# Re-pricing GpSimd's operations in the planner of a two-layer recurrent decoder step

## The chip, the cores and the metric

The kernel runs on one NeuronCore of a Trainium2 chip. TensorE multiplies matrices, VectorE (DVE), ScalarE (ACT) and GpSimd (POOL) do the elementwise work, and SyncE (SP) issues most of the transfers between device memory and the on-chip memory. Each engine runs its own instruction queue in order and waits on semaphores for the others. The metric is the device time of one execution in microseconds (us).

## The reference

The reference computes one inference step of a decoder trunk with two layers on 1024 prompt tokens and 8 x 4 sampled tokens, 1056 columns in all, with 1024 features. Everything is float32.

- Layer 0 is an RG-LRU layer: RMS norm, a projection to 2 x 1536 features (recurrent branch and gate), a causal convolution over 4 positions, two block-diagonal gate products with sigmoids, the recurrence h = a h + b over time, a multiplication by silu(gate), an output projection and the residual.
- Layer 1 is an HGRN2 layer: RMS norm, a projection to 4 x 1024 features (q, f, value, gate) for 8 heads, a gated linear recurrence with a 128 x 128 state per head, computed in chunks, a norm per head, a multiplication by silu(gate), an output projection and the residual.
- A final RMS norm follows. The outputs are the two activations and the new states of both layers.

## The kernel before

Activations are held transposed, features on the 128 partitions and tokens along the columns, in three chunks of 352 columns (`CH`). Every large product is made of three fp32r products (`mm3`, L243 to L245): an operand is split into a rounded part `hi` and the rest `lo`, and hi x hi, hi x lo and lo x hi are added up in PSUM. For each weight tile this takes a load (SP), a cast on ACT that makes `hi` (L378, and L1428 in `seven`) and a subtract that makes `lo`. That subtract runs on GpSimd nearly always (`subtract` with `e` as G, L323); activations get theirs from DVE mostly.

Layer 0 runs in the order: first products of gates and convolution inputs chunk by chunk while the inputs arrive (`begin`, `products`), then four groups of 384 recurrent features (`conv`, `gate`, `lru`, `split_y`) woven with the output products (`out`, `out_last`), and the first three products of layer 1 (`first1`). Layer 1 computes two heads with ordinary products and the other six with a seven-product scheme in place of eight (`seven`), whose combined operands are built on DVE, ACT and GpSimd where the layers meet (`build`: sums at L1368, casts at L1371, subtracts at L323). Each head has four bursts of small products (`burst1` to `burst4`): decay scalings of DVE (L1034, L1043, own gate L1064), 32-column products (L1052, L1106), transposes (L1161), states (L1217) and outputs (L1271, L1273). The end is the output projection, the final norm and the writing of the rows (`finish`: DVE L1701 for most rows, ACT and GpSimd L1699 for the last three of a block).

No instruction is issued where it is written. Each layer has one `Flow`: `fl.add` records an engine, an assumed duration, what is read and written, a priority and the code that emits it. The helpers `act`, `dve`, `pool` and `dma` compute the assumed duration from the number of columns n. `Flow.run` then simulates the queues. `plan` goes forward in time: at each step the engine that is free first takes, of its ready operations, the one with the least key. `back` goes backward from the end with the durations that the forward pass took and gives each operation its latest start, which is the next key. This alternates eight times (`TURNS`), and the plan with the earliest end is kept; for layer 0 the end is that of TensorE's last operation. For layer 0 `search` then tries 3000 random shifts of the keys of operations planned in the first 60 us, with a fixed seed, and keeps those that do not delay the first TensorE operation planned more than 20 us after that. Operations come out in the order of the kept plan, and with `manual_schedule` that is the order of each engine's queue. Large products are chained by `main=True`, so their order among themselves is fixed; small ones of layer 0 without it are placed by the plan. A `both` operation of DVE is planned to last until GpSimd's current operation ends and then nearly its own duration again, where GpSimd is busy at its start. The two layers are planned separately, each from an idle machine.

The change is in `pool`, L318 to L319. It sets the planned duration of weight and activation subtracts (L323), adds and squares in layer 0 (L428, L433, L582), gate maps (L720, L1010, L1012), masked values (L1195), the copies of a few columns and the last rows (L1699, L1735). The rsqrt operations on GpSimd (L447, L1299, L1670) have their own constants and do not go through it.

Of the kernel before, what the change touches and what calls it, by code (L numbers as in the profile page):

```python
# [211 lines left out]
def tile_trunk(ctx: ExitStack, tc: tile.TileContext, xT, prm, hc, w0, wg, wo0, w1, wo1, s_in,  # L212
# [83 lines left out]
    with ExitStack() as l0:  # L296
        pl = l0.enter_context(tc.tile_pool(name="l0", bufs=1, reuse_waits="tile"))
        fl = Flow("PE")
# [17 lines left out]
            fl.add("DVE", 0.13 + 0.0011 * n, emit, r, w, prio, both=both)  # L316

        def pool(n, emit, r, w, prio=5):  # L318
            fl.add("POOL", 0.1 + 0.00245 * n, emit, r, w, prio)  # L319

        def subtract(e, n, b, x, a, r, w, prio):

            emit = lambda: e.tensor_tensor(b, x, a.bitcast(F32), op=ALU.subtract)  # L323
            if e is G:
                pool(n, emit, r, w, prio)
            else:
                dve(n, emit, r, w, prio, True)
# [95 lines left out]
        def squares(k, x, xk, acc, eng=None, own=None, mult=False):  # L423

            a, ak = acc
            sq, sk = next(own or ts) if k else acc
            if mult:
                pool(CH, lambda: G.tensor_tensor(sq[:, :CH], x, x, op=ALU.mult), (xk,), (sk,), 2)  # L428
            else:
                act(CH, lambda: S.activation(sq[:, :CH], x, AF.Square), (xk,), (sk,), 2)  # L430
            if k:
                e = eng or G
                (pool if e is G else dve)(CH, lambda: e.tensor_tensor(a[:, :CH], a[:, :CH], sq, op=ALU.add), (sk, ak), (ak,), 2)  # L433
# [28 lines left out]
        def conv(g, head=False):  # L462

            items = []
            for j in range(3):
# [3 lines left out]
                def evac(c, ps, pk, by=None, j=j, m=m, mine=mine):  # L469
                    n = CH if c < 2 else 1024 - 2 * CH  # L470
                    if c == 0:
                        mine[0] = next(xbs)
                        pool(3, lambda xb=mine[0][0]: G.memset(xb[:, :3], 0.0), (), (mine[0][1],), 2)
                    elif head:
                        mine[c] = next(xbs)
                        pool(3, lambda xb=mine[c][0]: G.tensor_copy(xb[:, :3], tails[:, 4 * j:4 * j + 3]), (("tail", j),), (mine[c][1],), 0)
# [450 lines left out]
    with ExitStack() as l1:  # L927
        p1 = l1.enter_context(tc.tile_pool(name="l1", bufs=1, reuse_waits="tile"))
        fl = Flow(side=0.4)
# [637 lines left out]
        for k in range(H):  # L1567
            if k < 4:
                olds = [("x", 1, k, x) for x in range(2)] + [("T", 1, i, k, x) for i in range(2) for x in range(2)]
            else:  # L1570
                n, i = ((2, 0), (3, 0), (4, 0), (4, 1))[k - 4]
# [241 lines left out]
```

## Time and profile before

| | |
|---|---|
| time, median of 3 runs | 1061.05 us (1060.89 to 1061.98) |
| profiled execution: its time | 1062.88 us |
| profiled execution: span from first to last instruction | 1061.1 us |
| TensorE busy / weight loads busy | 1051.4 us (99%) / 1025.8 us (97%) |
| DVE / ACT / GpSimd busy | 843.7 us (80%) / 588.2 us (55%) / 542.0 us (51%) |
| mean granted TensorE clock | 0.995 |
| moved from and to device memory | 103.07 MB, mean 97 GB/s |

A row of a group reads: line, engine, operation, output <- inputs with their shapes, count | busy time, mean duration of one in ns | idle time of the engine before them and what ended it. A row of the time order reads: start, duration, engine, line, operation, tiles, count, and in brackets the idle time before it and what ended that. A row of the waits reads: who waited <- for whom: total us, times, longest. Lines are those of the kernel. PE is TensorE, PEld its weight loads.

### The profile page before, as it was taken

The page shows a single profiled execution, that of the slowest core. Times are in us where ns is not written, and L with a number is a line of the kernel's source. Part 1 is how long each engine was busy: PE and PEld are TensorE (multiplying, and loading weights), DVE is VectorE, ACT ScalarE, POOL GpSimd, SP SyncE. Part 2 cuts the span into 40 slices and gives each one's busy share as a digit, 9 for nine tenths or more (in the row PEclk, how much of TensorE's full clock was granted, in tenths as well). Part 3 has the DMA queues.
Part 4 walks back from the last instruction along what each step waited for, and adds up shares of the span by engine and source line. Part 5 has one row for each costly group of instructions (what it writes and reads, how often), then busy time and mean ns, then how long its engine had stood idle before and what let it go on. Part 6 is the DMA issues. An engine that isn't in the chain of part 4 may idle for free.

```text
span 1061.1 us, 25695 instructions
## 1 busy us (share of the span) xinstructions
PE 1051.4 (99%) x9972; PEld 1025.8 (97%) x9972; DVE 843.7 (80%) x1677; ACT 588.2 (55%) x1329; POOL 542.0 (51%) x604
## 2 busy tenths in 40 slices
PE   9999999999999999999999999999999999999997
PEld 9999999999999999999999999999999999999996
DVE  7999996888888689265799988978879797994435
ACT  6568656867675875243354474646464645652323
POOL 3425443444444455555677656555555565642544
PEclk9999999999999999999999999999999999999997
DMA  9201112123742685440210131312121212354204
GB/s 301 64 26 45 54 51 74 57 61 108 240 150 61 182 287 165 133 130 28 73 51 30 44 101 45 101 37 89 44 83 53 85 58 74 113 181 156 85 1 164
DMA packets 70121, 103.07 MB, mean 97 GB/s; under 512 B 9200, under 2 KB 51184, under 8 KB 70000
## 3 DMA queue, kind: packets, MB, share of 16 engines
q1 hardware_dynamic: 67696, 98.67, 29.9%
q10 hardware_dynamic: 2304, 2.77, 0.8%
q8 instruction: 78, 1.28, 0.5%
q14 instruction: 43, 0.35, 0.1%
HBM read 71.05 MB, written 25.49 MB: 91 GB/s over the span
## 4 chain that ended last, share of the span: by engine, by line
PE 89%; DVE 7%; POOL 1%; DMA 1%; issue 1%; ACT 0%; POOLq 0%; ACTq 0%; DVEq 0%
PE mm L243 24%; PE mm L244 24%; PE mm L245 24%; PE hg L567 1%; PE hg L1052 1%; PE hg L1161 1%; PE hg L1271 1%; DVE R L1368 1%; PE hg L1217 1%; PE hg L243 1%; PE hg L244 1%; PE hg L245 1%; PE hg L1273 1%; DMA wraw<-in_w_dram 1%; DVE tmp L1368 1%
## 5 line engine op out<-in xcount | busy, mean ns | idle before, releaser
L243 PE MATMUL mm<-xh,whi 128*128 128x352 f32 (+1 forms) x1143 | 358.8, 314 | 0.0
L245 PE MATMUL mm<-xh,wlo 128*128 128x352 f32 (+1 forms) x1143 | 353.4, 309 | 0.0
L244 PE MATMUL mm<-xl,whi 128*128 128x352 f32 (+1 forms) x1143 | 353.4, 309 | 0.0
L323 POOL TENSOR_TENSOR wlo<-wraw,whi 128x256 fp32r<-128x256 f32 (+3 forms) x184 | 203.2, 1121 | 178.7 <-ACT whi L378 79.9
L244 PEld LDWEIGHTS mm<-xl,whi 128*128 128x128 f32 x1143 | 215.3, 188 | 1.5
L243 PEld LDWEIGHTS mm<-xh,whi 128*128 128x128 f32 x1143 | 215.0, 188 | 1.5
L245 PEld LDWEIGHTS mm<-xh,wlo 128*128 128x128 f32 x1143 | 215.0, 188 | 0.0
L499 DVE SCALAR_TENSOR_TENSOR k<-xb,prm_sb,k 128x352 f32<-128x352 f32 (+2 forms) x144 | 90.0, 636 | 10.9 <-ACT k L496 7.7
L243 PE MATMUL mm<-t,whi 128*128 128x264 f32 (+1 forms) x306 | 89.4, 292 | 0.0
L244 PE MATMUL mm<-t,whi 128*128 128x264 f32 (+1 forms) x306 | 87.8, 287 | 0.0
L245 PE MATMUL mm<-t,wlo 128*128 128x264 f32 (+1 forms) x306 | 87.6, 286 | 0.0
L1501 DVE TENSOR_TENSOR k<-mm,k 128x264 f32<-128x264 f32 x144 | 60.2, 426 | 20.6 <-PE mm L245 17.5
L323 POOL TENSOR_TENSOR wlo<-R,whi 128x256 fp32r<-128x256 f32 x64 | 60.0, 957 | 24.7 <-ACT whi L1428 24.7
L582 POOL TENSOR_TENSOR k<-X 128x352 f32<-128x352 f32 x36 | 43.9, 1228 | 47.8 <-DVE R L583 38.2
L378 ACT CAST whi<-wraw 128x512 fp32r<-128x512 f32 (+2 forms) x83 | 46.1, 574 | 30.0 <-PE mm L244 15.7
L243 PEld LDWEIGHTS mm<-t,whi 128*128 128x128 f32 x306 | 57.7, 188 | 0.2
L245 PEld LDWEIGHTS mm<-t,wlo 128*128 128x128 f32 x306 | 57.8, 189 | 0.0
L244 PEld LDWEIGHTS mm<-t,whi 128*128 128x128 f32 x306 | 57.7, 189 | 0.0
L1428 ACT CAST whi<-wraw 128x512 fp32r<-128x512 f32 x52 | 32.1, 619 | 36.3 <-PE mm L245 16.8
L243 PE MATMUL mm<-yh,whi 128*128 128x352 f32 x153 | 50.0, 327 | 0.0
L245 PE MATMUL mm<-yh,wlo 128*128 128x352 f32 x153 | 49.4, 323 | 0.0
L244 PE MATMUL mm<-yl,whi 128*128 128x352 f32 x153 | 49.4, 323 | 0.0
(479 smaller groups left out, 2640.9 us busy)
## 6 DMA issues: line engine op xcount, KB each, us to landing
wraw<-in_w_dram SPq DMA_DIRECT2D x90, 256.0 KB, 2.8
wraw<-in_wo_dram SPq DMA_DIRECT2D x34, 192.0 KB, 2.6
si<-in_s_in_dram SPq DMA_DIRECT2D x8, 512.0 KB, 3.6
out_ss_out_dram<-si SPq DMA_DIRECT2D x8, 512.0 KB, 2.6
R<-in_w_dram SPq DMA_DIRECT2D x15, 256.0 KB, 2.6
sg<-x1b SPq DMA_DIRECT2D x21, 176.0 KB, 3.0
x<-sg SPq DMA_DIRECT2D x21, 176.0 KB, 1.9
R<-td SPq DMA_DIRECT2D x72, 44.0 KB, 2.0
```

Of the source, the lines that this page charges most:

```text
L243: T.matmul(out, wh, xh, start=first, stop=False)
L244: T.matmul(out, wh, xl, start=False, stop=False)
L245: T.matmul(out, wl, xh, start=False, stop=last)
L323: emit = lambda: e.tensor_tensor(b, x, a.bitcast(F32), op=ALU.subtract)
L378: act(m, lambda hi=hi, raw=raw, m=m: S.copy(hi[:, :m], raw[:, :m]), rk, (hk,), prio)
L499: dve(u, lambda src=src, dst=dst, sh=sh, k=k: V.scalar_tensor_tensor(dst, sh(src, k), pc("cw", 12 * k + m), dst, op0=ALU.mult, op1=ALU.add ...
L567: fl.add("PE", 0.62, lambda ps=ps, i=i, c=c: T.matmul(ps[:96, :CH], gs[:, i, :], ST[:96, chunk(c)], start=True, stop=True), (("gs",), *((" ...
L582: pool(CH, lambda x=x, a=a, b=b: G.tensor_tensor(x, a.bitcast(F32), b.bitcast(F32), op=ALU.add), (ak, bk), (xk,), 3)
L1052: T.matmul(ps[32 * j:32 * j + 32, n * w:n * w + w], B[:, o:o + 32], q(slice(o, o + 32)), start=True, stop=True, tile_position=(0, 32 * j))
L1368: dve(n, lambda: V.tensor_tensor(o, a, b, op=op), r, (w,), prio, True)
L1428: act(512, lambda: S.copy(hi, raw), (rk,), (hk,), 2)
L1501: dve(QT, lambda: V.tensor_tensor(o[0], z[0], u[0], op=ALU.add), (z[1], u[1]), (o[1],), 0)
```

## The change

One line in the helper that records a GpSimd operation. Below 96 columns the assumed duration stays at 0.1 + 0.00245 n us; from 96 columns on it is 0.42 + 0.00195 n us.

```diff
@@ -316,7 +316,7 @@
         def pool(n, emit, r, w, prio=5):
-            fl.add("POOL", 0.1 + 0.00245 * n, emit, r, w, prio)
+            fl.add("POOL", 0.1 + 0.00245 * n if n < 96 else 0.42 + 0.00195 * n, emit, r, w, prio)
```

No instruction, operand or buffer is changed. What can differ is the order of the instructions in each engine's queue, in both layers.

## The prediction

> **What bounds the kernel now.** I read the page first: busy shares, DMA shares and the chain that ended last.
>
> ```profile
> PE 1051.4 (99%) x9972; PEld 1025.8 (97%) x9972; DVE 843.7 (80%) x1677; ACT 588.2 (55%) x1329; POOL 542.0 (51%) x604
> PE 89%; DVE 7%; POOL 1%; DMA 1%; issue 1%; ACT 0%; POOLq 0%; ACTq 0%; DVEq 0%
> ```
>
> TensorE is 99% busy, weight loads fill 97%, and TensorE holds 89% of the chain. GpSimd, whose assumed durations change, is busy half the time and holds 1%. A busy matmul says little, since records overlap, so I looked at starts in the time order, for two waits of TensorE:
>
> ```profile
> 30.82 0.32 PE L244 MATMUL mm<-xl,yh 128*128 128x352 f32 x1
> 30.98 0.32 PE L245 MATMUL mm<-xh,yl 128*128 128x352 f32 x1
> 31.98 0.42 PE L243 MATMUL mm<-xh,yh 128*128 128x352 f32 x1 [0.68 <-DVE sg L527]
> ...
> 565.67 0.32 PE L245 MATMUL mm<-xh,wlo 128*128 128x352 f32 x1
> 566.42 1.44 PE L1052 MATMUL hg<-R,a 128*32 128x64 f32 x62 [0.43 <-DVE R L1064]
> ```
>
> Each record lasts 0.32 us, yet starts are 0.16 us apart. A stall therefore shows as the step beyond that: 1.00 us instead of 0.16 at 30.98, that is 0.84 lost, and 0.75 instead of 0.16 at 565.67, 0.59 lost. All that TensorE waited for in the whole span:
>
> ```profile
> PE hg L728 <- DVE ones L255: 1.0, 1, 1.0
> PE mm L243 <- DVE sg L527: 0.7, 1, 0.7
> PE hg L1106 <- DVE a L1034: 0.5, 1, 0.5
> PE hg L277 <- ACT sg L1726: 0.4, 1, 0.4
> PE hg L1052 <- DVE R L1064: 0.4, 1, 0.4
> ```
>
> Five waits, 3.0 us. The first is before the warm-up matmuls and no order changes it. That leaves 2.0 us: 0.7 in the start, 0.9 where the layers meet, 0.4 in the end. The stretches say the same (time, busy PE, PEld, DVE, ACT and POOL with counts, clock, DMA share, GB/s):
>
> ```profile
> 0.00:20.00 20.00, 18.97 (x134) 18.97 (x135) 14.91 (x34) 13.22 (x28) 7.54 (x13) 1.00 0.91 299
> ...
> 60.00:505.00 445.00, 445.00 (x2740) 438.56 (x2739) 347.42 (x602) 284.16 (x556) 211.53 (x233) 1.00 0.37 110
> 505.00:570.00 65.00, 63.95 (x804) 62.19 (x803) 57.19 (x100) 28.79 (x67) 47.35 (x43) 1.00 0.18 55
> 570.00:960.00 390.00, 390.00 (x5447) 376.74 (x5447) 339.55 (x738) 210.57 (x557) 216.26 (x250) 1.00 0.25 80
> ...
> 1045.00:1061.00 16.00, 9.27 (x56) 8.21 (x54) 6.63 (x16) 3.73 (x9) 5.67 (x7) 0.65 0.46 162
> ```
>
> For 835 of 1061 us (60 to 505, 570 to 960) TensorE has no gap at all. The stretches where the order can matter are the first 60 us (transfers at 0.91 of the engines), the meeting of the layers (DVE 57.19 of 65, GpSimd 47.35 of 65, its highest share), and the last 16.
>
> **The change part by part.** No instruction, tile or transfer is added or removed. One price in the planner changes: a GpSimd operation on n at least 96 columns is planned at 0.42 + 0.00195 n us instead of 0.1 + 0.00245 n. What moves is the position of instructions in each engine's queue, SP's loads among them, since the plan emits them all. Old price, new price and row:
>
> ```profile
> L323 POOL TENSOR_TENSOR wlo<-wraw,whi 128x256 fp32r<-128x256 f32 x104 | 93.9, 924 | 76.8 <-ACT whi L1428 62.1 <-DVE k L1501 14.6
> L323 POOL TENSOR_TENSOR wlo<-wraw,whi 128x512 fp32r<-128x512 f32 x58 | 83.3, 1443 | 87.3 <-ACT whi L378 65.3 <-DMA sg<-x 11.9 <-DVE X L505 3.9
> L582 POOL TENSOR_TENSOR k<-X 128x352 f32<-128x352 f32 x36 | 43.9, 1228 | 47.8 <-DVE R L583 38.2 <-DVE X L505 7.3 <-DVE nr L440 1.9
> L433 POOL TENSOR_TENSOR xb<-xb,k 128x352 f32<-128x352 f32 x21 | 20.4, 971 | 22.8 <-ACT k L430 22.6
> L1195 POOL TENSOR_TENSOR vb<-vst,bm 96x256 fp32r<-96x256 f32 x32 | 24.6, 785 | 25.0 <-DVE vst L1177 17.7 <-PE hg L1246 7.1 <-PE mm L1246 0.2
> ```
>
> At 256 columns 0.727 becomes 0.919 (measured 0.924); at 512, 1.354 becomes 1.418 (1.443); at 352, 0.962 becomes 1.106 (1.228 at L582). These prices improve. But L433 at 352 columns was right and becomes 0.14 too long, and L1195 moves from 0.06 short to 0.13 long. So one formula in n fits most of GpSimd's time and misfits some. An operation flagged `both` on DVE is also planned to stand still while GpSimd works, so longer GpSimd prices make the planned DVE slower as well.
>
> (1) The steady stretches, 60 to 505 and 570 to 960. TensorE waits for nothing, so no order can gain: 0. The cover is GpSimd's own earliness: the first row above shows 62.1 us of idling before 256-column subtracts because ACT had not yet cast, so those subtracts follow their input at once. If the cover went, a subtract run one place later would cost up to its own 0.92 us at the product that needs it. DVE has 50 us of air in 390. Bounds 0 to +0.9; I take 0.
>
> (2) The start. The search over the first 60 us draws from a fixed seed, but its draws fall on other neighbours once the planned times differ, so another order of loads is likely. A weight load and the transfer rate:
>
> ```profile
> wraw<-in_w_dram SPq DMA_DIRECT2D x90, 256.0 KB, 2.8
> ```
>
> 262,144 bytes at the 299 GB/s of the first stretch take 0.88 us. If the load that TensorE needs next falls behind one other, that is +0.88, ahead of one, -0.88; two such places bound it at -1.8 and +1.8. Nothing tells the sign, so I take 0. The casts and the subtracts follow their loads and count within that shift.
>
> (3) The wait on L527. DVE is late there after sums that run beside GpSimd; the queue of both around it:
>
> ```profile
> 26.88 2.69 DVE L433 TENSOR_TENSOR R<-R,xo 128x352 f32<-128x352 f32 x3
> 29.91 1.14 DVE L433 TENSOR_TENSOR R<-R,xo 128x352 f32<-128x352 f32 x2
> 30.98 0.52 DVE L527 TENSOR_TENSOR sg<-mm,R 128x352 f32<-128x352 f32 x1
> ...
> 26.86 1.69 POOL L323 TENSOR_TENSOR yl<-wraw,yh 128x512 fp32r<-128x512 f32 x1 [2.75 <-ACT yh L378]
> ```
>
> Three sums took 2.69 us while a subtract of 1.69 ran, two took 1.14 later. A plan that knows the subtract is longer may put L527 before sums that nobody needs yet. Between -0.7 (gone) and +0.7 (the same again) I take -0.35: this is the wait that the corrected price bears on most directly.
>
> (4) The meeting of the layers. Here DVE is the second limit. Rows of both engines:
>
> ```profile
> 538.58 0.67 DVE L1034 TENSOR_TENSOR sg<-sg 128x512 f32<-128x512 f32 x1
> 543.70 1.78 DVE L1034 TENSOR_TENSOR a<-a,sg 128x512 f32<-128x512 f32 x1
> ...
> 541.74 3.19 POOL L323 TENSOR_TENSOR wlo<-wraw,whi 128x512 fp32r<-128x512 f32 x2
> 564.10 0.82 POOL L1010 TENSOR_SCALAR ST<-k,smalls 128x352 f32<-128x352 f32 x1
> 564.91 2.42 POOL L1012 TENSOR_SCALAR a<-k,smalls 128x352 f32<-128x352 f32 x1
> ...
> 563.43 0.98 DVE L1368 TENSOR_TENSOR tmp<-xh,tmp 128x264 f32<-128x264 f32 x1 [1.10 <-POOL t L323]
> ```
>
> A 512-column multiply of DVE takes 0.67 us alone and 1.78 while GpSimd subtracts: 1.11 us for a collision. DVE's queue ahead of L1064 and L1034 holds the sums of the layer's operands, and behind it wait four scalings, the masks and the evacuations. Best case both waits vanish: -0.9. Worst case four scalings of one level that ran free collide: 4 x 1.11 = 4.4, less the 1.10 at 563.43, the only idle time that DVE shows between 520 and 570: +3.3. Repriced subtracts speak for the gain, a saturated DVE for a loss; I take 0.
>
> The Trainium skill, page "SBUF — State Buffer", section "Who interferes with whom", says that a DVE instruction with two SBUF inputs contends with a GpSimd instruction that reads SBUF, and that the one that comes second stands still for the whole of the other. The trace agrees as far as 0.67 against 1.78 shows it. By that rule a GpSimd duration belongs to a place and not to a size, no formula in n alone could aim better, and the -0.35 of (3) would be 0: 1062.88 - 1.83 = 1061.05 us instead of 1060.7.
>
> (5) Small products between the large ones. The planner places those of layer 0 (all of layer 1's but the last normalisation are chained). Switching costs as in the first row of a product after one:
>
> ```profile
> 541.22 0.43 PE L243 MATMUL mm<-xh,whi 128*128 128x352 f32 x1
> 541.49 0.32 PE L244 MATMUL mm<-xl,whi 128*128 128x352 f32 x1
> ```
>
> It starts 0.27 us before the next instead of 0.16, so a switch costs 0.11; one into a small product and one out of it make 0.22 for a place, an estimate. Three places joined or parted: -0.7 to +0.7; I take 0.
>
> (6) The end. On DVE two output multiplies stand before the last residual add, which all that follows waits for:
>
> ```profile
> 1047.95 1.11 DVE L1701 SCALAR_TENSOR_TENSOR R<-R,prm_sb,hg 128x376 f32<-128x376 f32 x2
> 1048.98 0.42 DVE L1724 TENSOR_TENSOR sg<-mm,sg 128x256 f32<-128x256 f32 x1
> 1055.20 2.09 POOL L1699 TENSOR_TENSOR sg<-sg 128x256 f32<-128x256 f32 x3 [3.13 <-ACT sg L1694]
> ```
>
> In front of them: -1.0; one more in front of it: +0.6. GpSimd's last three, 0.70 each, are now planned at 0.919, which is further off, but their order is fixed. I take 0.
>
> **The sum.** 0 + 0 - 0.35 + 0 + 0 + 0 = -0.35 us. The profiled execution took 1062.88 us for its span of 1061.1, and the median of the runs is 1061.05, so 1.83 comes off: 1062.88 - 0.35 - 1.83 = 1060.7 us. A measurement of this kernel can tell about 0.2%, 2.1 us, from no change.
>
> **The rivals.** A, faster: the better prices do what they say. The waits at L527, L1034 and L1064 vanish (1.6), the last add goes first (1.0), one load comes earlier (0.9): 1062.88 - 3.5 - 1.83 = 1057.5 us (1057.55). For it: GpSimd is in the chain right where TensorE waits (564.10, 564.91). Against it: it takes nearly every gap that exists, and two rows are priced worse.
>
> B, slower: collisions where the layers meet. The new order puts GpSimd's subtracts beside DVE's scalings; TensorE already waits 0.5 and 0.4 there, so beyond DVE's 1.10 us of idle time every microsecond of a collision goes into the span: +3.3, 1062.88 + 3.3 - 1.83 = 1064.4 us (1064.35). For it: DVE 57.19 of 65. Against it: the planner does count such collisions, now with longer GpSimd times. (The Trainium skill, page "SBUF — State Buffer", section "Who interferes with whom", states a lock that would do this.)
>
> C, slower: the start's new order puts two loads ahead of a needed one (1.8) and the wait on L527 doubles (0.7): 1062.88 + 2.5 - 1.83 = 1063.5 us. For it: the transfers are 0.91 busy there. Against it: the plan models the loads in both versions alike.
>
> D: the order barely moves, because every operand waits for the same casts and loads: 1061.05 us. Against it: a search with 3000 draws.
>
> **How the numbers follow.** Forecast (within 0.2%) 0.48, D 0.04, A 0.20, B 0.20, C 0.08. So faster 0.20, same 0.52, slower 0.28. The range reaches down to A, 1057.5, and up to B with one late load of the start, 1064.4 + 0.9 = 1065.3; some 7 in 100 lie below and 10 above.
>
> **What would show it.** (1) holds if TensorE's list of waits stays empty from 60 to 505 and from 570 to 960. (2): where the uninterrupted products begin, now here:
>
> ```profile
> 16.75 0.41 PE L243 MATMUL mm<-xh,whi 128*128 128x352 f32 x1
> ```
>
> (3): L527 in the list. (4): the waits between 505 and 570, and how many scalings take over 1.1 us. (6): the time from L1724's last add to the end. I am wrong if TensorE waits over 2 us in a stretch where it waits for nothing now, or if the start moves by more than two loads.

## The result and the profile after

The changed kernel takes 1076.8 us (median of 4 runs, 1075.88 to 1078.65) against 1061.51 us for the kernel before on the same chip. The ratio is 1.0146 with a 95% interval of 1.0129 to 1.0164. Its profiled execution took 1078.65 us, 15.77 more than the one before. The new prices cost 1.5% and gain nothing.

The engines did not get more to do. The page of the changed kernel, busy time and share of each engine:

```profile
PE 1056.5 (98%) x9972; PEld 1029.5 (96%) x9972; DVE 837.7 (78%) x1677; ACT 587.9 (55%) x1329; POOL 532.2 (49%) x604
```

GpSimd is busy 532.2 us where it was 542.0, and DVE 837.7 where it was 843.7. The instructions are the same, so the new order seems to leave the two less often in each other's way. TensorE gains nothing from it. What TensorE waits for in the changed kernel (who <- for whom: total us, times, longest):

```profile
PE mm L243 <- DVE sg L527: 3.4, 1, 3.4
PE mm L243 <- DVE k L1501: 2.7, 2, 1.5
PE mm L244 <- DVE xl L323: 2.3, 2, 1.9
PE mm L244 <- DVE xl L867: 1.3, 1, 1.3
PE hg L728 <- DVE ones L255: 1.0, 1, 1.0
PE mm L243 <- ACT xh L1371: 0.9, 1, 0.9
PE hg L1137 <- DVE sg L1034: 0.9, 1, 0.9
PE hg L453 <- DVE k L451: 0.7, 1, 0.7
```

A list of five lines and 3.0 us has become one of ten lines and 13.9 us (the two not shown are in the end, 0.4 and 0.3). Nearly all are for DVE, which is less busy than before: it is late, not overloaded. Stretches of the changed kernel (time; busy PE, PEld, DVE, ACT, POOL with counts; granted clock, DMA share, GB/s):

```profile
20.00:60.00 40.00, 35.50 (x205) 34.15 (x204) 36.19 (x79) 21.09 (x45) 14.66 (x18) 0.91 0.34 109
60.00:505.00 445.00, 445.00 (x2728) 438.44 (x2726) 342.70 (x609) 281.86 (x551) 208.55 (x229) 1.00 0.37 110
505.00:570.00 65.00, 65.00 (x742) 63.68 (x741) 53.44 (x97) 28.96 (x66) 40.63 (x39) 1.00 0.16 50
570.00:960.00 390.00, 383.61 (x5310) 369.56 (x5312) 331.65 (x720) 205.41 (x540) 211.21 (x252) 1.00 0.23 73
```

**Where the time goes.** The large products come in the same fixed order in both kernels, so the k-th of one can be set against the k-th of the other. Its start after minus its start before is the lag. Worked out in this way from the starts of the L243 products that write `mm` (the gate products of the same line write `hg` and change places), the lag is 1.5 us at the first, 8.9 at the product that started at 46.56 before, 10.1 at 504, 9.5 at 600, 15.3 at 650, 15.1 at 867, 17.0 at 1000, and 17.5 at the last. The span is only 15.6 longer. So about 9 us are lost in the first 47 us, 1 from there to 504, none where the layers meet, 6 between 600 and 650, 2 later, and the end gives 2 back. In the eight kernels below whose layer 0 is planned as before, the lag at 504 is -0.3 to 1.2 us, so a lag can be off by about 1 us from one execution to another.

**The start.** DVE and GpSimd of the changed kernel, then TensorE's late product (start, duration, engine, line, operation, tiles; in brackets the idle time before it):

```profile
20.20 3.25 DVE L433 TENSOR_TENSOR xb<-xb,xo 128x352 f32<-128x352 f32 x3
...
27.57 3.24 DVE L433 TENSOR_TENSOR R<-R,xo 128x352 f32<-128x352 f32 x4
...
30.73 0.41 DVE L448 TENSOR_TENSOR k<-ident,nr 128x256 f32<-128x256 f32 x1
...
36.50 0.95 DVE L527 TENSOR_TENSOR sg<-mm,R 128x352 f32<-128x352 f32 x2
...
28.79 1.64 POOL L323 TENSOR_TENSOR yl<-wraw,yh 128x512 fp32r<-128x512 f32 x1
...
33.36 0.32 PE L245 MATMUL mm<-xh,yl 128*128 128x352 f32 x1
37.07 0.66 PE L243 MATMUL mm<-xh,yh 128*128 128x352 f32 x1 [3.39 <-DVE sg L527]
```

The first norm of the kernel before spread its factor (L448) at 26.36; here that happens at 30.73, because the sums of squares in front of it were placed later. Everything behind it on DVE moves along: L527 comes at 36.50 instead of 30.98. The product at 37.07 is the same one that started at 31.98.

This wait has a second price. Five stretches of the changed kernel, clock third from the end:

```profile
33.40:37.00 3.60, 0.28 (x2) 0.00 (x0) 3.46 (x11) 1.18 (x4) 2.21 (x3) 0.81 0.26 75
37.00:38.00 1.00, 0.93 (x3) 0.93 (x4) 1.00 (x4) 0.93 (x2) 1.00 (x3) 0.50 0.80 231
...
41.00:42.00 1.00, 1.00 (x5) 1.00 (x5) 0.38 (x1) 0.48 (x1) 0.18 (x1) 0.50 0.03 10
42.00:43.00 1.00, 1.00 (x7) 1.00 (x6) 0.00 (x0) 0.00 (x0) 0.00 (x0) 0.78 0.17 45
43.00:44.00 1.00, 1.00 (x7) 0.84 (x6) 0.00 (x0) 0.00 (x0) 0.00 (x0) 1.00 0.00 0
```

After the wait TensorE runs at half its clock until about 42.4. Of the 5.4 us from 37.0 to there, half is lost: 2.7 us. The ledger of the lag at 46.6 is then 3.4 + 1.3 + 0.7 + 0.4 of waits (0.4 is the first of the two at `xl` L323), less the 0.7 that the kernel before waits at L527, and 2.7 of clock: 7.8 of 8.9 us.

The Trainium skill, page "TensorE: Matmul & The Clock Gate", section "Part 1: The HAM clock gate", says that the clock falls to half after at least one idle window of about 3.4 us and that the windows run freely. The trace agrees as far as the half rate and the length go: 0.50, over 6.8 us from about 35.6 on, which would be two windows. It does not show a wholly idle window: the wait began at 33.7, 1.9 us before the fall.

**The start of the seven-product scheme.** Before, DVE works through the sums of the combined operands (L1368, `xl` L323) nearly without idle time, and the first set is done soon after 619. The stretch, and the row of that last subtract in the time order:

```profile
600.00:616.00 16.00, 16.00 (x288) 14.89 (x287) 15.79 (x38) 9.52 (x34) 10.96 (x11) 1.00 0.23 83
```

```profile
619.43 0.43 DVE L323 TENSOR_TENSOR xl<-tmp,xh 128x264 fp32r<-128x264 f32 x1 [0.36 <-ACT xh L1371]
```

The same stretch of the changed kernel, which is there 9.5 us behind, with the one that follows, and then DVE and TensorE in the time order:

```profile
600.00:616.00 16.00, 16.00 (x126) 15.35 (x124) 13.01 (x25) 7.83 (x29) 13.65 (x16) 1.00 0.21 67
616.00:635.00 19.00, 15.27 (x277) 14.28 (x277) 16.77 (x42) 10.69 (x29) 5.38 (x6) 1.00 0.18 57
```

```profile
616.22 0.35 DVE L1253 SCALAR_TENSOR_TENSOR si<-si,gp,hg 128x128 f32<-128x128 f32 x1 [1.13 <-PE hg L1246]
621.99 0.43 DVE L1501 TENSOR_TENSOR k<-mm,k 128x264 f32<-128x264 f32 x1 [0.69 <-PE mm L245]
634.75 0.43 DVE L323 TENSOR_TENSOR xl<-tmp,xh 128x264 fp32r<-128x264 f32 x1
...
632.01 0.39 PE L243 MATMUL mm<-xh,whi 128*128 128x264 f32 x1 [0.92 <-ACT xh L1371]
634.29 0.39 PE L244 MATMUL mm<-xl,whi 128*128 128x264 f32 x1 [1.89 <-DVE xl L323]
```

DVE is idle 3.0 of the 16 us where it was idle 0.2 (0.3 over the same products, which the kernel before runs from 590.5 to 606.5). It stands before L1253 and L1501, which wait for TensorE, while sums are queued behind them that later, between 626 and 635, run without a wait of their own. So the sums are late, the first set ends at about 635, and TensorE is idle 3.7 us between 616 and 635.

**The end.** One stretch of the kernel before, one of the changed kernel, both over the last products:

```profile
1050.00:1053.00 3.00, 2.92 (x13) 2.92 (x14) 0.74 (x3) 0.53 (x2) 0.72 (x2) 0.50 0.88 319
```

```profile
1065.00:1068.00 3.00, 2.61 (x25) 2.53 (x24) 2.46 (x7) 1.80 (x4) 2.54 (x3) 1.00 0.70 252
```

In this execution of the kernel before, the clock falls to half in front of the last small products; in that of the changed kernel it falls after them. The 2.92 us that TensorE is busy there at half the clock would be 1.46 at the full one, so most of the 2 us come back by the clock and not by the plan.

### The profile page after: what moved, and what is told of

It reads as the page before. It is cut to its first block, busy times and chain, and to the rows that moved or that the text cites. A ratio compares the mean times of both kernels' runs of the same rounds, so it can differ in the third digit from the quotient of the medians.

```text
span 1076.7 us, 25659 instructions
## 1 busy us (share of the span) xinstructions
PE 1056.5 (98%) x9972; PEld 1029.5 (96%) x9972; DVE 837.7 (78%) x1677; ACT 587.9 (55%) x1329; POOL 532.2 (49%) x604
## 5 line engine op out<-in xcount | busy, mean ns | idle before, releaser
L243 PE MATMUL mm<-xh,whi 128*128 128x352 f32 (+1 forms) x1143 | 358.7, 314 | 0.9 <-ACT xh L1371 0.9
L323 POOL TENSOR_TENSOR wlo<-wraw,whi 128x256 fp32r<-128x256 f32 (+3 forms) x184 | 198.6, 1094 | 177.9 <-ACT whi L378 97.6
L243 PEld LDWEIGHTS mm<-xh,whi 128*128 128x128 f32 x1143 | 215.0, 188 | 2.8 <-ACT xh L1371 1.1
L499 DVE SCALAR_TENSOR_TENSOR k<-xb,prm_sb,k 128x352 f32<-128x352 f32 (+2 forms) x144 | 85.9, 606 | 17.4 <-ACT k L496 12.4
L243 PE MATMUL mm<-t,whi 128*128 128x264 f32 (+1 forms) x306 | 89.4, 292 | 2.7 <-DVE k L1501 2.7
L1501 DVE TENSOR_TENSOR k<-mm,k 128x264 f32<-128x264 f32 x144 | 59.0, 427 | 26.9 <-PE mm L245 25.3
L323 POOL TENSOR_TENSOR wlo<-R,whi 128x256 fp32r<-128x256 f32 x64 | 58.8, 940 | 27.0 <-ACT whi L1428 24.4
L243 PEld LDWEIGHTS mm<-t,whi 128*128 128x128 f32 x306 | 57.6, 188 | 3.3 <-DVE k L1501 1.7
L243 PE MATMUL mm<-yh,whi 128*128 128x352 f32 x153 | 51.3, 335 | 0.0
```

The costliest lines, as they stand in the source:

```text
L243: T.matmul(out, wh, xh, start=first, stop=False)
L499: dve(u, lambda src=src, dst=dst, sh=sh, k=k: V.scalar_tensor_tensor(dst, sh(src, k), pc("cw", 12 * k + m), dst, op0=ALU.mult, op1=ALU.add ...
L1501: dve(QT, lambda: V.tensor_tensor(o[0], z[0], u[0], op=ALU.add), (z[1], u[1]), (o[1],), 0)
```

## The experiments

`fl.until` is set for layer 0 alone, so it serves as the switch between the layers. "Clock" below is the time lost to a halved clock between 20 us and the last large products, worked out from stretches of 1 us as the sum of 1 minus the granted clock; the kernel before loses none there. It is an upper figure where a part of the fall lies in a wait.

**1. Which layer loses.** The new price in one layer, the old one in the other:

```diff
-            fl.add("POOL", 0.1 + 0.00245 * n, emit, r, w, prio)
+            fl.add("POOL", (0.1 + 0.00245 * n if n < 96 else 0.42 + 0.00195 * n) if fl.until else (0.1 + 0.00245 * n), emit, r, w, prio)
```

> The new prices in layer 0's plan alone, the old ones in layer 1's. Three theories stand. Counted twice: the new price is a mean that holds GpSimd's waiting for DVE (128x256 takes 0.73 us alone and 0.92 in the mean), while the plan charges the same collision to DVE once more, so the plan believes both engines fuller than they are. Redraw: any other prices give another order, and the kept constants suit one draw only. Longer GpSimd prices as such: GpSimd's work is placed later and arrives late. All three expect here the part of the loss that the changed kernel shows up to the meeting of the layers: its large products run 10.2 us behind there, so 1061.5 + 10 = 1071 us, 1068 to 1074. Below 1064 the loss would come from the joint of the two plans.

> The new prices in layer 1's plan alone. The rest of the loss: 1061.5 + 15.3 - 10.2 = 1066.6 us, 1064 to 1069, with TensorE's waits of 1 to 2 us where the seven-product scheme begins (before the fifth product of its first seven) and none in the first 60 us beyond those of before.

Layer 0 alone: 1070.64 us, ratio 1.0085 (1.007 to 1.010). Layer 1 alone: 1068.65 us, ratio 1.0063 (1.0046 to 1.008). The kernel before took 1062.0 beside them, so they lose 8.6 and 6.7 us, together 15.3, which is what the whole change loses. The place is the same as in the changed kernel: with layer 0 alone the lag is 7.9 at 46.6 and 9.2 at 504 and stays there; with layer 1 alone it is 1.2 until 504, 0 at 600 and 5.9 at 650. Where the layers meet neither loses.

**2. Is it counted twice?** A mean duration of GpSimd holds the time in which GpSimd stood behind DVE, and the `both` rule charges the same collision to DVE. This kernel has the new prices, and the lengthening is taken out of the planner:

```diff
-            if both and free["POOL"] > t0:
-                us = max(us, free["POOL"] - t0 + us - 0.13)
```

> The new prices in both plans, but the plan no longer lengthens a DVE operation that meets a busy GpSimd, so a collision is charged once, to GpSimd. Counted twice: the loss goes, 1060 to 1065 us. Redraw: another draw, no better than the changed kernel on average, 1068 to 1080. Longer GpSimd prices as such: no help, 1072 to 1080, since GpSimd's prices are the same.

1095.37 us, ratio 1.0318 (1.0302 to 1.0333), slower than any of the three ideas expected. Its three largest waits (its lines lie 2 lower):

```profile
PE hg L1050 <- DVE sg L1032: 8.4, 1, 8.4
PE mm L241 <- DVE k L1499: 6.9, 7, 1.8
PE mm L241 <- DVE sg L525: 3.8, 1, 3.8
```

So a longer price of GpSimd does not stand in for the collision rule. Without the rule the scalings where the layers meet are planned without the time that they stand behind GpSimd, and TensorE waits 8.4 us for one of them. If there is double counting, it is not mended from this side.

**3. Any other plan of the start.** Is the first 60 us worse because of the price, or because the old search result was one good draw? First the smallest change of price, in both layers, then the old price with another seed of the search, and without the search:

```diff
+            fl.add("POOL", 0.1 + 0.00245 * n if n < 96 else 0.11 + 0.00245 * n, emit, r, w, prio)
```

> The old prices with 0.01 us added to every GpSimd operation of at least 96 columns, a twentieth of what the change adds at 256 columns. Counted twice and longer prices as such: next to nothing, 1060 to 1064 us, since the sum of GpSimd's planned time hardly moves. Redraw: as slow as the changed kernel, 1068 to 1080, with waits in the first 60 us.

```diff
-        rng = Random(1)
+        rng = Random(2)
```

> The old prices everywhere, but the search over layer 0's first 60 us draws from seed 2 instead of 1; layer 1 is planned as before. Redraw by the search: 4 to 8 us slower, 1066 to 1070, all of it in the first 70 us, as in the run with 0.01 us added. Prices (even a small one tips the eight alternations of the plan, the search only polishes): no loss, 1061 to 1063.

```diff
-SEARCH = 3000
+SEARCH = 0
```

> The old prices, no search at all: the best of the eight alternations as it stands. Redraw by the search: the search of the kernel before is worth what a poor draw costs, so 4 to 8 us slower, 1066 to 1070. Prices tip the alternations: these are untouched here, so at most 2 us slower, 1061 to 1064.

A price longer by 0.01 us: 1068.34, ratio 1.0055 (1.0038 to 1.0072), 5.2 of its 6.5 us of lag there by 47 us. The other seed: 1066.12, ratio 1.0038 (1.0023 to 1.0053). No search: 1064.74, ratio 1.0022 (1.0012 to 1.0032). With no price changed at all, another draw of the start costs 2.4 to 3.8 us, so much of layer 0's loss has nothing to do with how good the prices are. The rest was asked with the new price in layer 0 under another seed and without the search, and with small changes of price in layer 0:

```diff
-        rng = Random(1)
+        rng = Random(3)
+            fl.add("POOL", (0.1 + 0.00245 * n if n < 96 else 0.42 + 0.00195 * n) if fl.until else (0.1 + 0.00245 * n), emit, r, w, prio)
```

> The new prices in layer 0 alone, as in the run that took 1070.64, with the search drawing from seed 3. A poor draw on top of a neutral price: the loss scatters about what other draws cost at the old prices (2.4 without the search, 3.8 with seed 2), so 1063 to 1067 us. A loss made by the prices: it stays, 1069 to 1073, with a wait of 2 us or more on L527.

```diff
-SEARCH = 3000
+SEARCH = 0
+            fl.add("POOL", (0.1 + 0.00245 * n if n < 96 else 0.42 + 0.00195 * n) if fl.until else (0.1 + 0.00245 * n), emit, r, w, prio)
```

> The new prices in layer 0 alone, without the search: the best of the eight alternations. At the old prices this cost 2.4 us. A poor draw: about the same, 1063 to 1066. A loss made by the prices: 6 us or more above the run at the old prices, 1069 to 1074.

```diff
+            fl.add("POOL", (0.1 + 0.00245 * n if n < 96 else 0.09 + 0.00245 * n) if fl.until else (0.1 + 0.00245 * n), emit, r, w, prio)
```

> Layer 1 as before; in layer 0 0.01 us is taken from every GpSimd operation of at least 96 columns. Redraw of the start (the size and sign of the shift do not matter): 4 to 8 us slower, 1066 to 1070, like the run with 0.01 us added. Longer prices do it: no loss beyond what another draw of the search costs, 1062 to 1065.

```diff
+            fl.add("POOL", (0.1 + 0.00245 * n if n < 96 else 0.12 + 0.00245 * n) if fl.until else (0.1 + 0.00245 * n), emit, r, w, prio)
```

> Layer 1 as before; in layer 0 0.02 us is added. Redraw: anything from 2 to 9 us slower, unrelated to the run with 0.01 us. Longer prices do it: as with 0.01 or more, 1067 to 1071.

| layer 0 | us | ratio | lag at 504 | clock lost |
|---|---|---|---|---|
| new price | 1070.64 | 1.0085 (1.007 to 1.010) | 9.2 | 1.7 |
| new price, seed 3 | 1069.03 | 1.0064 (1.0047 to 1.0081) | 5.1 | 0 |
| new price, no search | 1071.38 | 1.0086 (1.0071 to 1.0101) | 7.6 | 1.7 |
| old price + 0.01 (both layers) | 1068.34 | 1.0055 (1.0038 to 1.0072) | 6.0 | 1.7 |
| old price + 0.02 | 1067.44 | 1.0050 (1.0035 to 1.0065) | 5.2 | 0 |
| old price - 0.01 | 1066.16 | 1.0034 (1.0021 to 1.0047) | 4.5 | 1.7 |
| old price, seed 2 | 1066.12 | 1.0038 (1.0023 to 1.0053) | 3.9 | 0 |
| old price, no search | 1064.74 | 1.0022 (1.0012 to 1.0032) | 2.7 | 0 |

All eight are slower than the kernel before. The three with the new price cost 7.0 to 9.3 us by their medians, the five without it 2.4 to 6.3. So a redraw alone takes about half, and the price seems to add about 4 us (the means are 8.3 and 4.3). That second half is the weaker statement: part of the difference is the clock. Less the clock, the lags at 504 are 7.5, 5.1 and 5.9 us with the new price and 2.7 to 5.2 without it, so the groups overlap and their means differ by 2.4. The wait on L527 parts them better: 3.4, 3.0 and 2.4 us with the new price, 2.3 and 2.1 with + 0.01 and + 0.02, and none in the list with - 0.01, with seed 2 or without the search at the old price. So a longer price in layer 0 does seem to do something of its own, but eight draws do not show how much. How little decides about the clock is seen in a wait and a stretch of the kernel with the new price and seed 3, and then of the one with the new price and the old seed:

```profile
PE mm L243 <- DVE sg L527: 3.0, 1, 3.0
```

```profile
36.00:42.00 6.00, 6.00 (x40) 5.79 (x39) 5.77 (x14) 3.11 (x7) 1.08 (x3) 1.00 0.54 169
```

```profile
PE mm L243 <- DVE sg L527: 3.4, 1, 3.4
```

```profile
36.00:42.00 6.00, 5.00 (x21) 5.01 (x22) 5.28 (x13) 2.67 (x6) 2.45 (x4) 0.72 0.49 150
```

A wait of 3.0 us left the clock at 1.00; one of 3.4 brought it down, and so did 2.3 in the kernel with + 0.01, and in the one with - 0.01 two waits of 0.9 and 0.8.

**4. What a longer price does in layer 1.** A price acts on the plan in two ways: on the queue of GpSimd itself, and on the hold of DVE's `both` operations. Each alone, in layer 1 (`held` is when GpSimd's operation is taken to end in the hold alone; `...` stands for the conversion to the other price):

```diff
-            if both and free["POOL"] > t0:
-                us = max(us, free["POOL"] - t0 + us - 0.13)
+            if both and held > t0:
+                us = max(us, held - t0 + us - 0.13)
+            if e == "POOL":
+                held = t0 + ...
```

With the new price in `pool` for layer 1, and `held` by the old one:

> Layer 0 as before. In layer 1's plan GpSimd's own queue runs with the new prices, but a DVE operation that meets it is held only up to the end that the old price gives. Counted twice (the mean price is right for the queue and harmful where it holds DVE): no loss, 1061 to 1064 us. Longer GpSimd prices as such: the whole loss of layer 1's new prices, 1066 to 1070, with the waits before the fifth product of the first seven. In between, 1064 to 1066: both uses share it.

With the old price in `pool`, and `held` by the new one in layer 1:

> The complement: layer 0 as before, in layer 1 GpSimd's queue runs with the old prices, and a DVE operation that meets it is held up to the end that the new price gives. Counted twice: the loss is here, 1066 to 1070 us. Longer GpSimd prices as such: no loss, 1061 to 1064.

The queue at the new price and the hold at the old: 1067.13, ratio 1.0049 (1.0034 to 1.0064), of which up to 1.7 us is a fall of the clock at this wait:

```profile
PE hg L1108 <- DVE a L1036: 2.2, 1, 2.2
```

The hold at the new price and the queue at the old: 1064.86, ratio 1.0027 (1.0017 to 1.0036), no fall of the clock. Less the clock the two cost 3.1 and 2.6 us; the whole new price in layer 1 costs 6.6 with a fall of 1.7 in it, 4.9. So both ways cost, about alike, and the hold is not the whole of it. But they are not simply two parts of one loss. With the queue alone the lag grows where the layers meet (0.1 at 504, 2.6 at 600), where the whole new price loses nothing, and the waits before the fifth product that its expectation named do not come. With the hold alone the lag grows by 2.4 between 600 and 650, where the whole new price in layer 1 loses 5.9. Each price gives another order with waits of its own.

**5. Which price is right in layer 1.** First what an operation takes when nothing is in its way. Two rows of GpSimd and one of DVE in the kernel before, a subtract of 256 and one of 512 columns; beside the first DVE has no instruction with two SBUF inputs until 638.24 (the row shown), and beside the second none at all:

```profile
637.87 0.73 POOL L323 TENSOR_TENSOR wlo<-wraw,whi 128x256 fp32r<-128x256 f32 x1 [2.99 <-ACT whi L1428]
...
508.45 1.29 POOL L323 TENSOR_TENSOR wlo<-wraw,whi 128x512 fp32r<-128x512 f32 x1 [0.62 <-ACT whi L378]
...
638.24 0.92 DVE L1034 TENSOR_TENSOR sg<-a,sg 128x528 f32<-128x528 f32 x1
```

0.73 and 1.29 against means of 0.924 and 1.443. Of the 168 subtracts of 256 columns in the kernel before (L323), the 12 beside which DVE was busy less than 0.3 of the time took 0.73 on average, and the 125 beside which it was busy over 0.9 took 0.98. The old price for 256 columns was 0.727. It was the price of an undisturbed operation, and the new one is a mean with the disturbance in it. A line through such undisturbed durations (0.46 at 128 columns, 0.73 at 256, 1.29 at 512) is 0.167 + 0.0022 n. It was tried in layer 1 and in both layers, and beside it the old price + 0.10 and the new price for 256 columns alone:

```diff
+            fl.add("POOL", (0.1 + 0.00245 * n) if fl.until else (0.1 + 0.00245 * n if n < 96 else 0.167 + 0.0022 * n), emit, r, w, prio)
```

> Layer 0 as before; in layer 1 a formula fitted to GpSimd's durations where DVE is idle (0.731 us at 256 columns, 1.295 at 512): 0.167 + 0.0022 n from 96 columns on. Counted twice: this is the price that fits the plan's rule for collisions, so no loss, 1061 to 1063. Redraw: any other price draws another order, so 2 to 5 us slower. Longer prices as such: no loss either, since nothing is longer on the whole.

```diff
+            fl.add("POOL", 0.1 + 0.00245 * n if n < 96 else 0.167 + 0.0022 * n, emit, r, w, prio)
```

> Both layers with the formula fitted to GpSimd's durations where DVE is idle, 0.167 + 0.0022 n from 96 columns on (0.731 us at 256, 0.941 at 352, 1.294 at 512). Layer 1 loses nothing by it. Longer prices do it: these are shorter than the old ones from 268 columns on, so layer 0 loses at most a poor draw, 1062 to 1065. Redraw: 1066 to 1070.

```diff
+            fl.add("POOL", (0.1 + 0.00245 * n) if fl.until else (0.1 + 0.00245 * n if n < 96 else 0.20 + 0.00245 * n), emit, r, w, prio)
```

> Layer 0 as before; in layer 1 0.10 us is added to every GpSimd operation of at least 96 columns, half of what the change adds at 256 columns. A loss that grows with the price: between the 0.3 us that layer 1 lost at +0.01 and the 6.6 at the new prices, so 2 to 5 us slower, 1064 to 1067. Redraw: no relation with the size, anything from 0 to 8.

```diff
+            fl.add("POOL", (0.1 + 0.00245 * n) if fl.until else (0.919 if n == 256 else 0.1 + 0.00245 * n), emit, r, w, prio)
```

> Layer 0 as before; in layer 1 the new price for operations of 256 columns alone (0.919 instead of 0.727 us: the subtracts of the seven-product scheme's weights and the masked values), all others at the old ones. If the subtracts of the steady heads carry the loss of layer 1: 1066 to 1069. If it is the longer price of the sums' subtracts (264 columns) and of the 352- and 512-column work where the layers meet: 1061 to 1064.

The undisturbed price in layer 1: 1062.4 us, ratio 1.0001 (0.9991 to 1.001), no change. That speaks against the idea that any other price costs something in layer 1; it cannot tell double counting from prices that are too long, since nothing is longer on the whole. In both layers: 1066.54, ratio 1.0041 (1.0026 to 1.0056), which is again layer 0's redraw (lag 4.9 at 504 and 4.9 at the last product). + 0.10: 1066.23, ratio 1.0035 (1.0023 to 1.0047), 1.7 of it clock; it loses where the layers meet (the lag is -0.2 at 504 and 3.1 at 570), where the whole change loses nothing. The new price at 256 columns alone: 1064.02, ratio 1.0020 (1.001 to 1.003), 1.8 us; so as far as the parts add up, the other sizes carry the larger part of layer 1's loss.

**6. Are shorter prices free?** Up to here a plan could simply be better the less it expects. Two kernels with prices below the undisturbed duration, in layer 1:

```diff
+            fl.add("POOL", (0.1 + 0.00245 * n) if fl.until else (0.1 + 0.00245 * n if n < 96 else 0.00245 * n), emit, r, w, prio)
```

> Layer 0 is left as it was before; in layer 1 every GpSimd price is 0.10 us shorter than in the kernel before (0.632 us for 128x256 instead of 0.732), so that the plan takes GpSimd for faster than it is even when VectorE is idle (0.73). If the right price is the duration of an undisturbed instruction, a price below it costs as well: 2 to 5 us slower, 1064 to 1067. If only longer prices cost, because each lengthens the planned sums and so the planned gaps, this one costs nothing: 1061 to 1064.

```diff
+            fl.add("POOL", (0.1 + 0.00245 * n) if fl.until else (0.1 + 0.00245 * n if n < 96 else 0.00245 * n - 0.1), emit, r, w, prio)
```

> The same with 0.20 us taken off (0.532 us for 128x256), about as far below the undisturbed duration as the change's 0.919 lies above it. If the price has its best value at the undisturbed duration, this costs about as much as the change does in this layer: 5 to 9 us, 1067 to 1071. If only longer prices cost: 1061 to 1065.

They are not free, they are dearer: 1077.0 us, ratio 1.0146 (1.0129 to 1.0163), and 1086.82, ratio 1.0241 (1.0218 to 1.0264), 15.8 and 25.6 us by the medians. Both lie beyond even the expectation that a price too short costs as well. Waits of TensorE with - 0.10, and then the time order of DVE and GpSimd in front of the second of them:

```profile
PE mm L243 <- DVE k L1501: 4.8, 3, 2.1
PE hg L1052 <- DVE sg L1034: 3.4, 1, 3.4
```

```profile
539.45 1.23 DVE L1034 TENSOR_TENSOR R<-R,sg 128x512 f32<-128x512 f32 x1
540.61 1.75 DVE L1034 TENSOR_TENSOR sg<-sg 128x512 f32<-128x512 f32 x1
542.28 1.23 DVE L1034 TENSOR_TENSOR R<-R,sg 128x512 f32<-128x512 f32 x1
543.44 0.68 DVE L1034 TENSOR_TENSOR a<-sg 128x512 f32<-128x512 f32 x1
...
540.10 1.71 POOL L323 TENSOR_TENSOR wlo<-wraw,whi 128x512 fp32r<-128x512 f32 x1
541.77 1.20 POOL L323 TENSOR_TENSOR t<-R,t 128x264 fp32r<-128x264 f32 x1
```

The four scalings of one level take 4.89 us. In the kernel before, the first of the four starts at 537.98 and each takes 0.67, 2.68 together. GpSimd was not idle beside them there either:

```profile
537.80 3.28 POOL L323 TENSOR_TENSOR t<-R,t 128x264 fp32r<-128x264 f32 x1 [1.97 <-ACT t L1371]
```

The shortest subtract of this shape takes 0.75 us; this one lasted through all four scalings. So in the kernel before GpSimd did the waiting and TensorE lost nothing. With - 0.10 it is DVE that waits, in three of the four. TensorE needs the second of them: they start 1.5 us later and the first two take 1.6 longer, which makes 3.1 of the wait of 3.4, and TensorE itself is 0.3 us early. That a plan which takes GpSimd for faster than it is believes the subtracts to be over by then is the likely reason; the plan's own times are not in the trace. With - 0.20 the six waits at L1501 make 12.0 us and the longest at L1052 is 4.6. Of the two losses up to 5.1 and 8.5 us are clock.

By price in layer 1 the cost is then 25.6 us at - 0.20, 15.8 at - 0.10, 0.3 at the undisturbed line, 4.2 at + 0.10, and 6.6 for the change (+ 0.19 at 256 columns, + 0.06 at 512). So the best price tried lies at the old one or the duration without disturbance, and of the two 0.10 away the short one cost more. Each price is one order, though, and the orders lose at different places, so this is a trend of a few draws and no curve. No kernel that was tried beats the kernel before.

## Why the prediction was wrong

The forecast was 1060.7 us with a range to 1065.3; the kernel took 1076.8. The sign came out the other way through one judgement, the size through two bounds. In the terms of the sum, the start was taken as 0 within 1.8 and cost 8.9, the second steady stretch was bounded by 0.9 and cost 7.5, and the wait on L527, a part of the start, was taken as -0.35 and grew by 2.7.

**The step that failed first is the pricing in the change part:** "At 256 columns 0.727 becomes 0.919 (measured 0.924) ... These prices improve." It compared prices with means. The mean of a GpSimd operation holds its waits behind DVE, and the planner charges such collisions itself, through its `both` rule. The prediction named the other half, that longer GpSimd prices make the planned DVE slower as well, and gave it no term. The quantity to compare with was the undisturbed duration, 0.73 at 256 columns and 1.29 at 512, which the trace of before had in single rows. By these the old price is right to 0.01 at 256 columns and 0.06 long at 512, and the new one 0.19 and 0.13 too long. In layer 1 the undisturbed price costs nothing (1.0001), the new one 1.0063, and prices below it cost most. By this reading the step carries layer 1's 6.7 us and, of layer 0's 8.6, the part that a redraw does not. The sentence on the lock, that "a GpSimd duration belongs to a place and not to a size", was the right observation, and the prediction drew only 0.35 us from it. Rival A, the better prices that do what they say, falls with this step. What is not shown is that the double charge itself makes the bad order: with the hold alone layer 1 loses 2.6 us, with the queue alone 3.1 without its fall of the clock, so a queue of GpSimd that is planned too long hurts by itself, though at another place than the whole new price. How a longer price leads to the worse order stays open.

**(1) The steady stretches**, bounds 0 to +0.9. From 60 to 505 no wait came, as forecast, though the lag grew from 8.9 at 46.6 to 10.1 at 504, a little over the bound. From 570 to 960 it failed: the lag grows from 9.5 at 600 to 17.0 at 1000, eight times the bound. The reasoning was that a place without a wait has nothing to gain, and that one subtract late costs at most its own 0.92 us. But DVE's queue is in order, and the plan put a whole group of sums behind adds (L1501) that wait for TensorE. A stretch without waits is one where the present order fits; it says nothing of how far a new order can miss.

**(2) The start**, bounds -1.8 to +1.8, priced by loads. The lag at 46.6 is 8.9 us. Nothing of it is two late loads: the product at 16.75, the prediction's own sign for this term, came 0.3 us earlier, the waits are for DVE, whose sums come in another order, and 2.7 us are the clock. The prediction's own remark that the search draws afresh was the mechanism of about half of it, but it was priced as a shift of loads with a sign that could go either way. Five other redraws all cost, 2.4 to 6.3 us, so the order of the kernel before is a good draw. Rival C named the place and had 2.5 us.

**(3) The wait on L527**, taken as -0.35: it went from 0.7 to 3.4 us. The upper bound, "the same again", had no ground in a row: nothing limits how many of the sums that nobody needs yet a new order puts in front of L527, and it came at 36.50 instead of 30.98.

**(4) The meeting of the layers** came out right. Both waits are gone, the lag goes from 10.1 at 504 to 9.5 at 600, which lies within -0.9 to +3.3. This was in part luck: with + 0.10, between the old price and the new one, the lag grows by 3.3 at this place, and with - 0.10 by 5.3, the clock included. The price of a collision was also read wrongly. The scaling of 0.67 us that the prediction calls alone ran beside the subtract of 3.28 us shown above, so its "four scalings of one level that ran free" were already in a collision, and GpSimd paid for it. What an order decides here is which of the two engines waits. Rival B did not come to pass, though its collisions did, as DVE's rows of the changed kernel for the same level show:

```profile
545.94 1.60 DVE L1034 TENSOR_TENSOR R<-R,sg 128x512 f32<-128x512 f32 x1
547.47 1.78 DVE L1034 TENSOR_TENSOR sg<-sg 128x512 f32<-128x512 f32 x1
549.17 0.68 DVE L1034 TENSOR_TENSOR R<-R,sg 128x512 f32<-128x512 f32 x1
```

Two scalings take 1.60 and 1.78 us, and TensorE does not wait for them. With the price of - 0.10 the like happens at the same place, later against the large products, and there TensorE waits 3.4 us. So a collision has a price only where the result is due.

**(5) Small products.** They were not measured by themselves. Between 47 and 504 us of the kernel before, where TensorE has no waits in either kernel, the lag moves between 6.3 and 11.8 us, and the difference of its ends is 1.2, outside the term's -0.7 to +0.7. That a place of small products costs for a while and gives it back is the likely reason of the swings.

**(6) The end**, bounds -1.0 to +0.6: in these two executions it gave 2 us back, most of it because the clock fell later. No row of the prediction looked at the clock, though the stretch 1045 to 1061 was quoted with a clock of 0.65.

**What is left over.** The waits listed make 10.9 us more than before, less the 0.3 in the end, and the clock 2.7: 13.3 of the 17.5 us of lag at the last product. A wait in the list is about 0.16 us shorter than the step it makes in the starts (33.36 to 37.07 is 3.71, less the usual 0.16 is 3.55, shown as 3.39), which makes 1 us for the six waits that are more. The remaining 3 us are spread over steps too small for the list and were not assigned.

## What to carry to other kernels

A duration in a profile holds the waits of its place; a planner that models a collision did best here with the duration of the operation alone. A price set to the mean cost, and a price below that duration cost more. A short row of one engine does not mean that nothing ran beside it: look whether the other engine's row is long there. An order that a search has found for one set of numbers is a draw: before judging a change of the numbers, redraw with the old ones (another seed, no search, a hundredth of a microsecond) and see what that costs by itself. And a stretch without waits bounds the gain of a reordering, not its loss.

## What was not expected of the hardware

- The clock multiplies waits. One fall lasted 3.4 us at half the clock, which is 1.7 us where TensorE has work all through it, as in the kernels with the new price in layer 1 alone and with + 0.10. With - 0.10 the slow time is three times as long, with - 0.20 five times. It is not decided by the longest wait: a fall followed a longest wait of 0.9 us (layer 0, - 0.01) and none a wait of 3.0 (new price, seed 3). The four runs of that last kernel took 1066.44, the profiled one without a fall, and 1068.85 to 1069.32; that the others had the fall is likely from the size and from their mean granted clocks, 0.995 to 0.997 against 0.999, and no trace shows it. The Trainium skill, page "TensorE: Matmul & The Clock Gate", section "HAM oscillation", gives as the rule that TensorE should have no idle gap over about 3.4 us; these runs show that much shorter gaps bring the clock down too.
- GpSimd's subtract of 128x256 takes 0.73 us undisturbed and up to 2.36 in the kernel before, its time for 512 columns goes from 1.27 to 2.27, and that for 264 columns from 0.75 to 3.28. The Trainium skill, page "SBUF — State Buffer", section "Who interferes with whom", states that the one that comes second stands still for the whole of the other. The rows of the four scalings agree in kind (0.68 alone, 1.23 to 1.75 beside subtracts of 1.20 and 1.71).
